# Scores of two attention maps as interleaved 64-row products into two banks, in place of stacked 128-row products

## The chip, the cores and the metric

The kernel runs on one core of one Trainium2 chip. A core has five engines that run their own queues in order and wait for one another through semaphores: PE (TensorE: matmuls, with its weight loads shown apart as PEld), DVE (VectorE), ACT (ScalarE), POOL (GpSimd) and SP (which issues most transfers here). Matmuls write to PSUM, a memory of eight banks of 128 x 512 f32. The metric is the device time of one execution in microseconds (us).

## What is computed

One block of an encoder, on 512 positions of width 1024, in f32. The part that the change touches is the scores of two attentions:

```
# A: 8 heads of 64, chunk-causal with a clipped relative bias per head
scores = einsum(q, k) / sqrt(64) + bias ; probs = softmax(scores) ; o_a = probs @ v
# B: 4 heads, each with two maps of 64 dimensions
s1 = einsum(qa, k1) * scale ; s2 = einsum(qb, k2) * scale
w  = softmax(mask(s1)) - lam * softmax(mask(s2)) ; out = w @ v   (then an RMS norm)
# around them
proj = x @ w_in ; merged = gates * branches ; x = LN1(alpha x + merged @ w_out)
x = LN2(alpha x + relu(x @ w_ff1)^2 @ w_ff2)
```

So a pair of maps is either two heads of A (a head pair p, heads 2p and 2p+1) or the two maps of one head of B. Each map has a contraction of only 64.

## The kernel before

Every f32 operand of a large product is split into a high part, rounded to the matmul type, and a low part, the remainder, and a product is the sum of three matmuls: high by high, high by low, low by high (smm and tmm, L177 to L185). These wide products, 512 columns each, are nearly all of PE's work.

The attention runs inside the projections. `proj` (L647) is a generator that issues the projections in steps; `attn_a` (L328) and `attn_b` (L497) are generators of attention steps, and the loop at L681 to L692 takes one step of attention and then one or two steps of projection. The Tile framework's scheduler then fixes the order of instructions on every engine at build time; at run time each queue is strictly in that order.

A unit of attention is one map and one block t of 128 query rows. Chunk-causality leaves n = 128 (t+1) key columns, so a score matmul has 128, 256, 384 or 512 columns. The chain of a unit: scores on PE into a bank (L266 to L272); DVE adds the bias and takes the row minimum of the negated sum (L278); ACT takes exp and the row sum (L280); DVE the reciprocal (L282); POOL multiplies by it (L372 in A; L575 for the second map in B); three units later PE transposes the block into a bank (L289), ACT copies it as high part ph (L296), DVE forms the low part pl (L297); after the last block of a map the product with v follows (L351 and L352 in A, L511 to L513 in B).

Scores use stacked operands. `stack` (L248) turns a bank that holds 64 rows of one map over 64 rows of another into two tiles: for map e, one half holds the high part and the other half the low part, so a tile of 128 rows is [high; low] of one map. That takes two ACT and two DVE instructions on 64 rows each (L254, L255). `swapped` (L260) makes [low; high] of a q tile by two transfers from SBUF to SBUF (L262, L263). Then scores of one map are two matmuls over all 128 rows: [high; low] by [high; low], and [low; high] by [high; low] (L270, L271), which sum all four products.

The banks (L72): four "mm" for the wide products, one "o" for products with v, and three "st", which both the scores and the transposes of A take in turn (B's transposes go to an mm bank). Later stages use all eight in rotation (L700, L846).

POOL also turns q and k of B by their positions (`rope`, L476 to L485, four instructions for each head and side).

Of the kernel before, what the change touches and what calls it, by code (L numbers as in the profile page):

```python
# [16 lines left out]
P = 128  # L17
S = 512
# [22 lines left out]
def block_kernel(ctx, tc, w, x_t, x, pos, relb, bgate, lq1, lk1, lq2, lk2, subg,  # L41
# [30 lines left out]
    def bank(tag):  # L72
        return psum.tile([P, S], F32, tag=tag, bufs={"mm": 4, "st": 3, "o": 1}[tag], name=name(tag))
# [174 lines left out]
    def stack(ps, scale):  # L248
        res = []
        for e in range(2):  # L250
            t = qp.tile([P, S], FR, tag="q", name=name("q"))
            hs = slice(64 * e, 64 * e + 64)
            ls = slice(64 - 64 * e, 128 - 64 * e)
            A.activation(t[hs], ps[hs], AF.Copy, scale=scale)  # L254
            V.scalar_tensor_tensor(out=t[ls], in0=ps[hs], scalar=scale,  # L255
                                   in1=t[hs].bitcast(F32), op0=ALU.mult, op1=ALU.subtract)
            res.append(t)
        return res

    def swapped(q):  # L260
        t = qp.tile([P, S], FR, tag="q", name=name("q"))
        nc.sync.dma_start(out=t[0:64].bitcast(F32), in_=q[64:128].bitcast(F32))  # L262
        nc.sync.dma_start(out=t[64:128].bitcast(F32), in_=q[0:64].bitcast(F32))  # L263
        return t

    def scores(q1, q2, k1, t):  # L266
        n = (t + 1) * P
        sl = slice(t * P, n)
        ps = st_bank()
        T.matmul(ps[:, :n], q1[:, sl], k1[:, :n], start=True, stop=False)  # L270
        T.matmul(ps[:, :n], q2[:, sl], k1[:, :n], start=False, stop=True)  # L271
        return ps  # L272
# [55 lines left out]
    def attn_a():  # L328
        units = []
        for p in range(4):  # L330
            for e in range(2):
                for t in range(NT):
                    units.append((p, e, t))
# [3 lines left out]
        def finish(u, ex, r):  # L337
            p, e, t = u
            n = (t + 1) * P
# [24 lines left out]
        for i in range(len(units) + LAG + 1):  # L364
            if i < len(units):
                p, e, t = units[i]
                q1, q2, k1 = qk_a[p]
                h = 2 * p + e
                ps = scores(q1[e], q2[e], k1[e], t)
                ex, r = softexp(ps, tbias[h], t)  # L370
                n = (t + 1) * P
                G.tensor_scalar(ex[:, :n], ex[:, :n], r, None, op0=ALU.mult)  # L372
                pend.append((units[i], ex, r))
                if e == 1 and t == NT - 1:
                    qk_a.pop(p)
# [610 lines left out]
```

## Time and profile before

| | |
|---|---|
| median of 3 runs (lowest, highest) | 741.46 us (741.35, 741.72) |
| the profiled execution, its own time | 741.43 us |
| its span in the trace | 739.6 us |
| PE busy | 725.7 us, 98% of the span, 3446 matmuls |
| PEld busy | 606.0 us, 82% |
| DVE busy | 423.4 us, 57% |
| ACT busy | 283.6 us, 38% |
| POOL busy | 94.4 us, 13% |
| granted TensorE clock over the span | 0.997 of full speed |
| transfers q<-q of `swapped` | 32, 128 KB each, 2.3 us median to landing |

How to read it: the profile shows one execution. A matmul's own duration overlaps the next one's, so what a matmul takes from PE is read from the start of one to the start of the next, here called its pitch. A busy engine is not one at its peak, and idle time of an engine that nobody waits for costs nothing. The attention lies between 42 and about 300 us, inside the projections; after that come the branch products, the output product, the two layer norms and the feed-forward part.

### The profile page before, as it was taken

The numbers are of one execution on the slowest core, as the hardware profiler recorded it, in microseconds if no ns is written. First come the engines' busy times: TensorE is split into PE (matmuls) and PEld (weight loads), VectorE is DVE, ScalarE is ACT, GpSimd is POOL, SyncE is SP. The second block draws the span as 40 slices with busy tenths as digits, with TensorE's granted clock in tenths as the row PEclk, the third lists the DMA queues.
The fourth block names the chain that finished last, engine by engine and source line by source line (L and its number), as shares of the span: only waits on it lengthen the run. The fifth ranks groups of instructions, "written<-read, shape, count | busy, mean of one in ns | idle before, by whom it ended". The sixth has DMA issues, their size and how long they took to land.

```text
span 739.6 us, 9267 instructions
## 1 busy us (share of the span) xinstructions
PE 725.7 (98%) x3446; PEld 606.0 (82%) x3446; DVE 423.4 (57%) x831; ACT 283.6 (38%) x497; POOL 94.4 (13%) x127
## 2 busy tenths in 40 slices
PE   8999999999999999999999999999999999999995
PEld 6888888878888888888788888888888888888885
DVE  6566655546666764746876886423135655612545
ACT  5565654536565643224363223221212322312200
POOL 0023333550122121143000000000000000000001
PEclk9999999999999999999999999999999999999998
DMA  8553222212332222182502232322223223232302
GB/s 294 197 173 112 85 88 60 83 58 86 121 108 86 86 63 104 62 313 96 190 1 84 87 114 86 115 86 98 102 86 113 86 86 113 86 113 86 115 29 85
DMA packets 26940, 78.34 MB, mean 106 GB/s; under 512 B 4368, under 2 KB 5136, under 8 KB 26896
## 3 DMA queue, kind: packets, MB, share of 16 engines
q1 hardware_dynamic: 26176, 76.71, 31.3%
q10 hardware_dynamic: 720, 1.05, 0.4%
q8 instruction: 27, 0.44, 0.2%
q14 instruction: 17, 0.14, 0.1%
HBM read 71.45 MB, written 2.10 MB: 99 GB/s over the span
## 4 chain that ended last, share of the span: by engine, by line
PE 87%; DVE 4%; POOL 3%; ACT 2%; DMA 2%; issue 1%; SPq 0%; DVEq 0%; ACTq 0%; POOLq 0%
PE mm L178 11%; PE mm L180 11%; PE mm L179 11%; PE mm L183 7%; PE mm L185 7%; PE mm L184 7%; PE st L185 3%; PE st L184 3%; PE st L183 3%; PE st L180 3%; PE st L179 3%; PE st L178 3%; POOL G L629 2%; DMA raw<-in_w_dram 2%; PE st L271 1%; PE o L185 1%
## 5 line engine op out<-in xcount | busy, mean ns | idle before, releaser
L83 DVE TENSOR_TENSOR wl<-raw,wh 128x1024 fp32r<-128x1024 f32 (+1 forms) x115 | 140.2, 1219 | 128.5 <-ACT wh L82 128.4
L82 ACT CAST wh<-raw 128x1024 fp32r<-128x1024 f32 (+1 forms) x115 | 120.0, 1044 | 207.6 <-PE st L185 67.1
L183 PE MATMUL mm<-wh,X 128*128 128x512 f32 (+1 forms) x192 | 77.0, 401 | 1.9 <-ACT X L82 1.6
L178 PE MATMUL mm<-X,wh 128*128 128x512 f32 x192 | 76.9, 401 | 0.0
L179 PE MATMUL mm<-X,wh 128*128 128x512 f32 x192 | 74.9, 390 | 0.0
L180 PE MATMUL mm<-X,wl 128*128 128x512 f32 x192 | 74.9, 390 | 0.0
L184 PE MATMUL mm<-wl,X 128*128 128x512 f32 (+1 forms) x192 | 74.5, 388 | 0.0
L185 PE MATMUL mm<-wh,X 128*128 128x512 f32 (+1 forms) x192 | 74.2, 388 | 0.0
L783 POOL TENSOR_SCALAR s<-s 128x1 f32<-128x1 f32 x1 | 0.4, 409 | 388.8 <-DVE s L767 388.8
L178 PE MATMUL mm<-x1t_h,wh 128*128 128x512 f32 x128 | 49.8, 389 | 0.0
L179 PE MATMUL mm<-x1t_l,wh 128*128 128x512 f32 x128 | 49.8, 389 | 0.0
L180 PE MATMUL mm<-x1t_h,wl 128*128 128x512 f32 x128 | 49.8, 389 | 0.0
L280 ACT ACTIVATE e<-e,s 128x128 f32<-128x128 f32 (+3 forms) x64 | 36.1, 564 | 30.4 <-DVE s L278 30.0
L372 POOL TENSOR_SCALAR e<-e,s 128x128 f32<-128x128 f32 (+3 forms) x32 | 34.7, 1085 | 76.3 <-DVE s L282 76.3
L183 PEld LDWEIGHTS mm<-wh,X 128*128 128x128 f32 x192 | 36.2, 189 | 9.8 <-ACT X L82 2.7
L185 PEld LDWEIGHTS mm<-wh,X 128*128 128x128 f32 x192 | 36.0, 188 | 7.8 <-DVE X L83 0.3
L180 PEld LDWEIGHTS mm<-X,wl 128*128 128x128 f32 x192 | 36.0, 188 | 7.7
L178 PEld LDWEIGHTS mm<-X,wh 128*128 128x128 f32 x192 | 36.1, 188 | 6.9
L184 PEld LDWEIGHTS mm<-wl,X 128*128 128x128 f32 x192 | 36.2, 188 | 6.7 <-DVE wl L83 0.2
L179 PEld LDWEIGHTS mm<-X,wh 128*128 128x128 f32 x192 | 36.2, 188 | 6.5
L82 ACT CAST V<-lt 128x512 fp32r<-128x512 f32 x24 | 14.9, 621 | 62.8 <-DVE lt L858 62.8
L180 PE MATMUL st<-x1t_h,wl 128*128 128x512 f32 (+1 forms) x104 | 38.8, 373 | 0.0
(257 smaller groups left out, 1537.0 us busy)
## 6 DMA issues: line engine op xcount, KB each, us to landing
raw<-in_w_dram SPq DMA_DIRECT2D x119, 512.0 KB, 3.3
q<-q SPq DMA_DIRECT2D x32, 128.0 KB, 2.3
G<-in_relb_dram SPq DMA_DIRECT2D x8, 256.0 KB, 4.2
x<-in_x_dram SPq DMA_DIRECT2D x4, 512.0 KB, 7.6
e<-in_x_t_dram SPq DMA_DIRECT2D x7, 256.0 KB, 6.4
out_dram<-x SPq DMA_DIRECT2D x3, 256.0 KB, 2.0
out_dram<-x ACTq DMA_DIRECT2D x3, 256.0 KB, 2.1
raw<-in_w_dram SPq DMA_DIRECT2D x2, 256.0 KB, 3.2
```

The source lines that it names most:

```text
L82: A.copy(out=h, in_=src)
L83: (eng or V).tensor_tensor(out=l, in0=src, in1=h.bitcast(F32), op=ALU.subtract)
L178: T.matmul(ps, lw_h, rh, start=first, stop=False)
L179: T.matmul(ps, lw_h, rl, start=False, stop=False)
L180: T.matmul(ps, lw_l, rh, start=False, stop=last)
L183: T.matmul(ps, ah, w_h, start=first, stop=False)
L184: T.matmul(ps, ah, w_l, start=False, stop=False)
L185: T.matmul(ps, al, w_h, start=False, stop=last)
L271: T.matmul(ps[:, :n], q2[:, sl], k1[:, :n], start=False, stop=True)
L280: A.activation(e[:, :n], e[:, :n], AF.Exp, bias=nm, scale=-1.0, accum_out=sums)
L372: G.tensor_scalar(ex[:, :n], ex[:, :n], r, None, op0=ALU.mult)
L629: G.tensor_tensor(out=m, in0=m, in1=g, op=ALU.add)
```

## The change

The scores are written on plain tiles. `parts_of` replaces `stack`: one ACT instruction makes the high part of all 128 rows (map 0 in rows 0 to 63, map 1 in rows 64 to 127) and one DVE instruction the low part. `swapped` and its transfers are gone. `scores` now makes both maps of a pair in one call: three products per map (high by high, high by low, low by high), each over 64 rows, issued in turn, map 0, map 1, map 0 and so on, map 0 into one bank of a new kind "sc" and map 1 into the other. A pair therefore takes six matmuls where it took four. The three st banks become two sc banks and one st bank, which the transposes of A have to themselves.

The order of units in A changes with it: both heads of a pair run together, block by block, and two units are issued at every second step; the product with v comes ahead of the transposes in a step.

```diff
-        return psum.tile([P, S], F32, tag=tag, bufs={"mm": 4, "st": 3, "o": 1}[tag], name=name(tag))
+        return psum.tile([P, S], F32, tag=tag, bufs={"mm": 4, "sc": 2, "st": 1, "o": 1}[tag], name=name(tag))
...
-    def stack(ps, scale):
-        res = []
-        for e in range(2):
-            t = qp.tile([P, S], FR, tag="q", name=name("q"))
-            hs = slice(64 * e, 64 * e + 64)
-            ls = slice(64 - 64 * e, 128 - 64 * e)
-            A.activation(t[hs], ps[hs], AF.Copy, scale=scale)
-            V.scalar_tensor_tensor(out=t[ls], in0=ps[hs], scalar=scale,
-                                   in1=t[hs].bitcast(F32), op0=ALU.mult, op1=ALU.subtract)
-            res.append(t)
-        return res
-
-    def swapped(q):
-        t = qp.tile([P, S], FR, tag="q", name=name("q"))
-        nc.sync.dma_start(out=t[0:64].bitcast(F32), in_=q[64:128].bitcast(F32))
-        nc.sync.dma_start(out=t[64:128].bitcast(F32), in_=q[0:64].bitcast(F32))
-        return t
-
-    def scores(q1, q2, k1, t):
+    def parts_of(ps, scale):
+        h, l = (qp.tile([P, S], FR, tag="q", name=name("q")) for _ in range(2))
+        A.activation(h, ps, AF.Copy, scale=scale)
+        V.scalar_tensor_tensor(out=l, in0=ps, scalar=scale, in1=h.bitcast(F32),
+                               op0=ALU.mult, op1=ALU.subtract)
+        return h, l
+
+    def scores(q, k, t):
+
         n = (t + 1) * P
         sl = slice(t * P, n)
-        ps = st_bank()
-        T.matmul(ps[:, :n], q1[:, sl], k1[:, :n], start=True, stop=False)
-        T.matmul(ps[:, :n], q2[:, sl], k1[:, :n], start=False, stop=True)
+        ps = [bank("sc") for _ in range(2)]
+        for i, (a, b) in enumerate(((0, 0), (0, 1), (1, 0))):
+            for m in range(2):
+                hs = slice(64 * m, 64 * m + 64)
+                T.matmul(ps[m][:, :n], q[a][hs, sl], k[b][hs, :n], start=(i == 0), stop=(i == 2))
         return ps
...
-        units = []
-        for p in range(4):
-            for e in range(2):
-                for t in range(NT):
-                    units.append((p, e, t))
+        units = [(p, t, e) for p in range(4) for t in range(NT) for e in range(2)]
...
-            if i < len(units):
-                p, e, t = units[i]
-                q1, q2, k1 = qk_a[p]
-                h = 2 * p + e
-                ps = scores(q1[e], q2[e], k1[e], t)
-                ex, r = softexp(ps, tbias[h], t)
+            if i < len(units) and i % 2 == 0:
+                p, t, _ = units[i]
                 n = (t + 1) * P
-                G.tensor_scalar(ex[:, :n], ex[:, :n], r, None, op0=ALU.mult)
-                pend.append((units[i], ex, r))
-                if e == 1 and t == NT - 1:
+                for e, ps in enumerate(scores(*qk_a[p], t)):
+                    ex, r = softexp(ps, tbias[2 * p + e], t)
+                    G.tensor_scalar(ex[:, :n], ex[:, :n], r, None, op0=ALU.mult)
+                    pend.append((units[i + e], ex, r))
+                if t == NT - 1:
                     qk_a.pop(p)
+            k = i - LAG - 1
+            if k >= 0 and units[k][1] == NT - 1:
+                p, t, e = units[k]
+                pv(p, e)
             if i >= LAG and i - LAG < len(units):
                 finish(*pend.pop(0))
-            k = i - LAG - 1
-            if k >= 0 and k % NT == NT - 1:
-                p, e, t = units[k]
-                pv(p, e)
             yield
...
-            res.append(stack(ps, 0.125 if which == 0 else 1.0))
-        q1, k1 = res
-        return q1, [swapped(q) for q in q1], k1
+            res.append(parts_of(ps, 0.125 if which == 0 else 1.0))
+        return res
...
-                q1, q2, k1 = ops[h]
-                es = []
-                for m in range(2):
-                    ps = scores(q1[m], q2[m], k1[m], t)
-                    es.append(softexp(ps, maskb, t))
-                (e1, r1), (e2, r2) = es
+                (e1, r1), (e2, r2) = [softexp(ps, maskb, t) for ps in scores(*ops[h], t)]
...
-            r = stack(ps, 0.125 if which == 0 else 1.0)
-            if which == 0:
-                qk_a[p] = [r, [swapped(q) for q in r], None]
-            else:
-                qk_a[p][2] = r
+            qk_a.setdefault(p, []).append(parts_of(ps, 0.125 if which == 0 else 1.0))
```

What stands in the queues, at two places. The first is on PE, at the last block (t = 3) of the last head pair of A, among the wide products of the v projection of B. Names are tiles: q are parts of queries and keys, st, sc, mm and o banks, e a block of probabilities. Before:

```order
L185 MATMUL mm_1575<-wh_1580,X_225 128x512
L270 MATMUL st_1661<-q_941,q_854 128x512
L271 MATMUL st_1661<-q_941,q_860 128x512
L289 MATMUL st_1674<-ident,e_1561 128x128
L351 MATMUL o_1678<-ph_1517,V_327 128x512
```

In the changed kernel, at the same block:

```order
L263 MATMUL sc_1615<-q_912,q_819 128x512
L263 MATMUL sc_1616<-q_912,q_819 128x512
L263 MATMUL sc_1615<-q_913,q_819 128x512
L263 MATMUL sc_1616<-q_913,q_819 128x512
L263 MATMUL sc_1615<-q_912,q_820 128x512
L263 MATMUL sc_1616<-q_912,q_820 128x512
L281 MATMUL st_1639<-ident,e_1448 128x128 x2
L183 MATMUL mm_1576<-wh_1582,X_218 128x512
```

One map's two matmuls became a run of six for two maps, and the transposes behind them go to the one st bank. Of 32 calls, 30 are such a run of six; two are cut by wide products.

The second place is on POOL, where the last units of A meet the rotations of B (L480 to L485 before, L465 to L470 after, four rows for each of eight tiles G). Before, the multiply of the unit (head 7, t = 0) stands among them and those of t = 1 to 3 behind:

```order
L480 TENSOR_TENSOR s_2487<-G_1184,cos_t 128x128
L481 TENSOR_TENSOR s_2488<-G_1184,sin_t 128x8x8
L372 TENSOR_SCALAR e_1561<-e_1561,s_1566 128x128
L483 TENSOR_TENSOR s_2488<-G_1184,sin_t 128x8x8
L485 TENSOR_TENSOR G_1184<-s_2487,s_2488 128x8x16
L480 TENSOR_TENSOR s_2493<-G_1491,cos_t 128x128
L481 TENSOR_TENSOR s_2494<-G_1491,sin_t 128x8x8
L483 TENSOR_TENSOR s_2494<-G_1491,sin_t 128x8x8
L485 TENSOR_TENSOR G_1491<-s_2493,s_2494 128x8x16
L372 TENSOR_SCALAR e_1599<-e_1599,s_1604 128x256
```

In the changed kernel:

```order
L465 TENSOR_TENSOR s_2469<-G_1175,cos_t 128x128
L357 TENSOR_SCALAR e_1554<-e_1554,s_1559 128x384
L466 TENSOR_TENSOR s_2470<-G_1175,sin_t 128x8x8
L468 TENSOR_TENSOR s_2470<-G_1175,sin_t 128x8x8
L470 TENSOR_TENSOR G_1175<-s_2469,s_2470 128x8x16
L465 TENSOR_TENSOR s_2475<-G_1490,cos_t 128x128
L466 TENSOR_TENSOR s_2476<-G_1490,sin_t 128x8x8
L468 TENSOR_TENSOR s_2476<-G_1490,sin_t 128x8x8
L470 TENSOR_TENSOR G_1490<-s_2475,s_2476 128x8x16
L357 TENSOR_SCALAR e_1562<-e_1562,s_1567 128x384
```

The rotations kept their places; the multiply among them is now one of 384 columns (head 6, t = 2), and the next one of 384 columns (head 7, t = 2) stands behind the last rotation, with the two of t = 3 after it.

## Rows read from the trace of the kernel before

**Rows 1.** The page: busy time by engine, and the chain that ended last, by engine.
```profile
PE 725.7 (98%) x3446; PEld 606.0 (82%) x3446; DVE 423.4 (57%) x831; ACT 283.6 (38%) x497; POOL 94.4 (13%) x127
...
PE 87%; DVE 4%; POOL 3%; ACT 2%; DMA 2%; issue 1%; SPq 0%; DVEq 0%; ACTq 0%; POOLq 0%
```

**Rows 2.** Windows: stretch, length, PE, PEld, DVE, ACT, POOL busy, clock, DMA share.
```profile
42.00:140.00 98.00, 97.71 (x491) 82.09 (x490) 61.09 (x157) 55.44 (x129) 32.77 (x32) 1.00 0.31 96
140.00:180.00 40.00, 38.29 (x190) 31.10 (x189) 22.45 (x53) 19.85 (x43) 16.97 (x33) 1.00 0.27 79
180.00:300.00 120.00, 120.00 (x604) 101.86 (x603) 75.45 (x208) 64.02 (x129) 23.87 (x21) 1.00 0.28 88
```

**Rows 3.** Timeline of POOL and PE where A ends and the rotations run.
```profile
140.67 0.46 POOL L480 TENSOR_TENSOR s<-G,cos_t 128x128 f32<-128x128 f32 x1 [0.81 <-ACT G L467]
...
151.32 0.60 POOL L372 TENSOR_SCALAR e<-e,s 128x128 f32<-128x128 f32 x1
...
154.36 3.69 POOL L372 TENSOR_SCALAR e<-e,s 128x256 f32<-128x256 f32 x3
...
151.98 0.33 PE L289 MATMUL st<-ident,e 128*128 128x128 f32 x1 [1.25 <-POOL e L372]
```

**Rows 4.** Timeline of PE: start us, duration us; score matmuls of each width.
```profile
58.48 0.33 PE L270 MATMUL st<-q,q 128*128 128x384 f32 x1
58.65 0.34 PE L271 MATMUL st<-q,q 128*128 128x384 f32 x1
58.83 0.60 PE L289 MATMUL st<-ident,e 128*128 128x128 f32 x4
...
62.02 0.39 PE L270 MATMUL st<-q,q 128*128 128x512 f32 x1
62.25 0.39 PE L271 MATMUL st<-q,q 128*128 128x512 f32 x1
...
66.61 0.22 PE L270 MATMUL st<-q,q 128*128 128x128 f32 x1
66.67 0.28 PE L271 MATMUL st<-q,q 128*128 128x128 f32 x1
66.78 0.41 PE L289 MATMUL st<-ident,e 128*128 128x128 f32 x2
66.95 0.48 PE L178 MATMUL mm<-X,wh 128*128 128x512 f32 x1
67.27 0.39 PE L179 MATMUL mm<-X,wh 128*128 128x512 f32 x1
...
69.77 0.28 PE L270 MATMUL st<-q,q 128*128 128x256 f32 x1
69.88 0.28 PE L271 MATMUL st<-q,q 128*128 128x256 f32 x1
70.00 0.49 PE L289 MATMUL st<-ident,e 128*128 128x128 f32 x3
```

**Rows 5.** Timeline of the weight loads: eight loads of 128 columns, merged.
```profile
226.75 0.97 PEld L524 LDWEIGHTS mm<-ones,e 128*128 128x128 f32 x8
```

**Rows 6.** Groups by shape: the same weight loads; busy us, mean ns of one.
```profile
L524 PEld LDWEIGHTS mm<-ones,e 128*128 128x128 f32 x32 | 4.0, 191 | 0.1
```

**Rows 7.** Groups by shape: POOL's multiply of 384 columns.
```profile
L372 POOL TENSOR_SCALAR e<-e,s 128x384 f32<-128x384 f32 x8 | 10.0, 1245 | 15.7 <-DVE s L282 15.7
```

**Rows 8.** Timeline: one transpose of A, and when its bank is read out.
```profile
128.93 0.49 PE L289 MATMUL st<-ident,e 128*128 128x128 f32 x3
...
129.97 0.56 DVE L297 TENSOR_TENSOR pl<-st,ph 128x384 fp32r<-128x384 f32 x1 [0.41 <-ACT ph L296]
```

**Rows 9.** Groups by shape: the weight split on DVE; the copies of `stack`.
```profile
L83 DVE TENSOR_TENSOR wl<-raw,wh 128x1024 fp32r<-128x1024 f32 x113 | 138.8, 1229 | 125.0 <-ACT wh L82 124.8
...
L254 ACT ACTIVATE q<-mm 64x512 fp32r<-64x512 f32 x32 | 18.9, 590 | 13.6 <-DVE q L255 9.6 <-PE st L271 2.0 <-PE mm L180 1.1
...
L255 DVE SCALAR_TENSOR_TENSOR q<-mm,q 64x512 fp32r<-64x512 f32 x32 | 22.0, 689 | 4.5 <-ACT q L254 3.5
```

More of the change, by code (lines that the diff above doesn't have):

```diff
@@ L337, in finish @@
         def finish(u, ex, r):
-            p, e, t = u
-            n = (t + 1) * P
+            p, t, e = u
             if t == 0:
@@ L699, in block_kernel @@
     early.close()
-    rotation[:] = ["mm", "mm", "mm", "mm", "o", "st", "st", "st"]
+    rotation[:] = ["mm", "mm", "mm", "mm", "o", "sc", "sc", "st"]
     late = ctx.enter_context(tc.tile_pool(name="late", bufs=1))
@@ L845, in block_kernel @@
         pass
-    rotation[:] = ["o", "st", "st", "st", "mm", "mm", "mm", "mm"]
+    rotation[:] = ["o", "sc", "sc", "st", "mm", "mm", "mm", "mm"]
     def x1t(k, lo=0, hi=S):
```

## The prediction, made before the changed kernel was run

> **What bounds the kernel now.** I read the page first, then windows over the attention stage, then the timeline of PE there, and last POOL's timeline at the one place where PE waits. The page shows PE busy for 98% of the span and 87% of the chain that ended last, with DVE at 57%, ACT at 38% and POOL at 13% [rows 1]. So the time is the sum of PE's pitches plus the moments in which PE stands still. The windows say how many of those there are in the stretch that the change touches: PE is busy 97.71 of 98 us from 42 to 140, 38.29 of 40 from 140 to 180 and all of 120 from 180 to 300 [rows 2], so it stands still for 0.3 + 1.7 = 2.0 us. Of these, 1.25 us are one wait for POOL at 151.98, where a transpose wants the block whose multiply stands among the rotations [rows 3]. The clock is granted in full in all three stretches [rows 2], so it has no part in the sum. Everything after 300 us keeps its instructions, and PE is in order, so what the attention stage gains or loses moves the end by as much.
>
> The reader should see from this that removing ACT or DVE work pays next to nothing, and that the change has to be costed in PE pitches.
>
> **What the scores take now.** Pitch is start to start [rows 4]. A map with 128 columns takes 66.78 - 66.61 = 0.17 us for its two matmuls, one with 256 takes 0.23, with 384 takes 0.35, with 512 takes twice 62.25 - 62.02, 0.46. The four blocks of a map take 1.21 us, two maps 2.42 us, and there are eight such pairs (four head pairs of A, four heads of B): 19.4 us in all. This is the whole stake on PE.
>
> A wide matmul hides the load of the next one's weights, a narrow one does not: eight loads in a row, with almost no columns behind them, are 0.97 us from the first start to the last end [rows 5], and one alone shows 0.19 [rows 6], so they follow each other every (0.97 - 0.19) / 7 = 0.11 us. That is the pitch of 256 columns.
>
> **The change part by part.** *The matmuls.* A pair of maps takes six instead of four, over 64 rows each. No row of this kernel has a matmul on less than 128 rows, so the price has to be bounded by what the two halves of the array do at the same time. There are three cases, all from the same pitches.
>
> (a) Both the columns and the loads of the two halves overlap. Then six matmuls are three rounds: 3 x 0.11, 3 x 0.115, 3 x 0.175 and 3 x 0.23 for the four widths, 1.89 us in place of 2.42, a gain of 0.53 x 8 = 4.2 us.
>
> (b) The columns overlap, the loads follow each other. Six loads are 6 x 0.11 = 0.67 us, which is more than the three rounds for 128, 256 and 384 columns and about the same for 512 (0.69). The sum is 3 x 0.67 + 0.69 = 2.70 us, a loss of 0.28 x 8 = 2.2 us. The narrow blocks lose more than the wide ones win.
>
> (c) Nothing overlaps: twice case (a), 3.78 us, a loss of 1.36 x 8 = 10.9 us.
>
> I take (b). In the trace, loads never stand closer than 0.11 us [rows 5, 6], and a wide matmul hides exactly one; six separate loads with little to hide them is what these rows are nearest to.
>
> The Trainium skill speaks on both sides here. TensorE: Matmul & The Clock Gate, section LDWEIGHTS, says that a load takes its columns at 1.2 GHz and no less for fewer rows, 107 ns for 128 columns; the trace agrees for 128 rows (0.11), and no run here shows 64. TensorEngine Tiling (Array Packing), section Key Properties, says that tiles of the array load weights and multiply in parallel, which is case (a). By the first page alone the sum would be (b), by the second it would be (a).
>
> *The change between 128 and 64 rows.* PE now goes from whole-array to half-array work and back around each of 33 stretches of scores (two calls are cut by wide products, so a few more). The nearest row is the other change of mode in this kernel: after transposes the next wide matmul has a pitch of 67.27 - 66.95 = 0.32 instead of 0.23 us, 0.09 more, and going into the transposes costs nothing (a score matmul of 384 columns keeps its 0.18 ahead of them) [rows 4]. In the new order 25 stretches are followed directly by transposes, which pay this 0.09 today already. The other eight add 8 x 0.09 = 0.7 us. The lower bound is 0. The upper one is that PE must run empty each time: a 512-column matmul lasts 0.39 us at a pitch of 0.23 [rows 4], so 0.16 us, 66 times, 10.6 us. I take 0.7, the row nearest to it.
>
> *POOL's place among the rotations.* The rotations keep their places, but the block that waits among them is now 384 columns wide and a second one stands behind them. If the multiply starts at the same 151.32 as today's [rows 3], it ends 1.25 us later [rows 7] at 152.57, where today's 0.60 ended at 151.92: 0.65 us later. PE comes there earlier: between the end of the k projection and this transpose stand 36 wide products before and after; the scores there take 0.67 + 0.69 = 1.36 us in place of 1.21, the transposes ahead are five blocks in place of nine (0.4 us less), so 0.2 us earlier. The wait grows from 1.25 to about 2.1 us. The next multiply follows the other rotations, which took 154.36 - 151.92 = 2.44 us, and ends at 152.57 + 2.44 + 1.25 = 156.3. PE is there after three transposes and twelve wide products, 3.1 us after 152.6, at 155.7, and waits 0.5. Together 2.6 in place of 1.25: +1.4 us. In case (a) PE is 0.15 us earlier still, +1.5; in case (c) a microsecond later, +0.3.
>
> *One st bank for the transposes of A.* A bank is read out 129.97 + 0.56 - 128.93 = 1.6 us after its transpose starts [rows 8]. In the new order at least twelve wide products, 2.75 us, lie between two transposes, so 1.1 us is left over. One weight split on DVE that comes ahead of the read-out takes 1.2 us [rows 9], which uses that up and little more. I take 0, with 2 us as the upper end if two splits line up at several of the 32 turns; then the wide products behind the transpose in PE's queue wait, and with them everything. The sc banks have some 24 wide products, 5.5 us, between calls in most of A: 0.
>
> *The copies and transfers.* 16 ACT instructions of 0.59 and 16 DVE instructions of 0.69 us go [rows 9], 9 and 11 us of engines that PE hardly waits for: 0, and at best the 0.75 us of still PE that is not POOL's wait [rows 2, 3]. The 32 transfers of `swapped` free SP's queue, where weight loads stand behind them; PE does not wait for those weights now [rows 2]: 0.
>
> **The sum** is made against the profiled execution's own 741.43 us, which is the median (741.46) to within 0.03. +2.2 (scores) + 0.7 (change of mode) + 1.4 (POOL) + 0 + 0 = +4.3 us: 745.7 us.
>
> **The rivals.** *Faster: the two halves work independently, loads too* (case (a), change of mode free). -4.2 + 1.5 = -2.7 us: 738.7. For it: the two halves share no rows and no bank, so nothing in the program makes one wait for the other. Against it: the loads in the trace are never closer than 0.11 us [rows 5, 6]. It decides from the point at which two loads take under about 0.17 us together: there the scores cost no more than today with the change of mode paid. POOL's wait eats a third of it. Chance 0.27.
>
> *The halves don't overlap at all*, so the change does not do what it says: +10.9 + 0.7 + 0.3 = +11.9 us, 753.3. For it: the pitches of this kernel's matmuls are those of one queue, each starting when the columns of the one before are through [rows 4]. Against it: all of those use every row of the array, so they could not have overlapped, and the rows don't speak of halves. Chance 0.15.
>
> *PE runs empty at every change between 64 and 128 rows.* As in case (b) plus 10.6 us, with POOL's wait hidden by most of a microsecond in return: +2.2 + 10.6 + 0.6 = +13.4 us, 754.8; with overlapping loads 6.4 us less, 748.4. Against it: the change to transposes costs 0.09 us, not 0.16 twice [rows 4]. The Trainium skill, TensorEngine Tiling (Array Packing), section Key Properties, states such a drain for a change of tiling mode; no row of this kernel can show it. Chance 0.20.
>
> **How the numbers follow.** Forecast 0.38, faster rival 0.27, no overlap 0.15, running empty 0.20. What a measurement of this kernel tells from no change is 0.2%, 1.5 us, so 740.0 to 742.9 is the same. The forecast reaches from 741.5 (no price for the mode, no more wait for POOL) to 749 (the st bank and more of the mode): of its 0.38, 0.02 faster, 0.06 same, 0.30 slower. The faster rival, from 737.2 (POOL's wait hidden) to 741.5: 0.20 faster, 0.07 same. The others are slower whole. Faster 0.22, same 0.13, slower 0.65. The range 737.5 to 756.0 leaves out a sliver of the faster rival and the upper half of running empty with loads in turn, under 0.2 together.
>
> **What would show it.** In the trace of the changed kernel, the starts of six score matmuls of 512 columns: two starts close together and then about 0.23 us until the next two for (a) and (b), an even 0.23 for (c). For 128 columns the whole run of six decides between (a), 0.33 us, and (b), 0.67. The pitch from a wide product into the first score matmul, and from the last one out, against 0.23 shows the price of the mode. The wait for POOL of the transpose of head 6, t = 2 should be about 2.1 us and that of head 7 about 0.5; transposes of A that wait for DVE would show the st bank. The copies on ACT and DVE should be 16 each at 0.6 and 0.7 us, and nobody should gain from the other 16. The prediction is wrong if loads of 64 rows stand closer than those of 128, which is the faster rival, or if the change of mode costs more than a tenth of a microsecond.

## The result, and the profile after

The changed kernel takes 752.84 us (median of 4 runs, 751.21 to 753.94), the kernel before 741.58 us in the same session (741.35 to 741.72): a ratio of 1.015, 95% interval 1.0134 to 1.0167. It is slower, as forecast, but by 11.3 us where 4.3 were forecast. The profiled execution of the changed kernel is its shortest, 751.21 us, 9.8 us more than that of before; its span in the trace is 749.2 us.

The page of the changed kernel (busy us, share, instructions; the chain that ended last, by engine) answers to [rows 1]:

```profile
PE 733.5 (98%) x3510; PEld 599.2 (80%) x3510; DVE 411.3 (55%) x815; ACT 274.9 (37%) x481; POOL 94.9 (13%) x127
...
PE 87%; POOL 4%; DVE 3%; DMA 2%; ACT 2%; issue 1%; SPq 0%; DVEq 0%; ACTq 0%; POOLq 0%
```

PE has 64 products more and is 7.8 us longer busy; ACT and DVE have 8.7 and 12.1 us less to do, and nobody gains by that. The windows of the changed kernel (columns as in [rows 2]):

```profile
42.00:140.00 98.00, 97.97 (x508) 76.59 (x507) 53.85 (x147) 50.11 (x118) 31.64 (x32) 1.00 0.23 76
140.00:180.00 40.00, 36.96 (x185) 28.45 (x183) 21.08 (x44) 18.85 (x38) 18.01 (x32) 1.00 0.19 56
180.00:300.00 120.00, 119.60 (x615) 95.58 (x616) 69.00 (x209) 59.72 (x125) 24.47 (x22) 1.00 0.22 74
```

PE hardly stands still between 42 and 140 us, so the one st bank costs nothing there; it stands still for 3.0 us instead of 1.7 where the rotations run, and for 0.4 us behind 180 us, where it did not before. Next, PE's timeline of the changed kernel around stretches of scores (start us, duration us; x6 is the six half products of a call, merged), which answers to [rows 4]:

```profile
46.08 0.62 PE L263 MATMUL sc<-q,q 64*128 64x256 f32 x6
46.63 0.50 PE L178 MATMUL mm<-X,wh 128*128 128x512 f32 x1
46.97 0.40 PE L179 MATMUL mm<-X,wh 128*128 128x512 f32 x1
...
58.68 0.39 PE L179 MATMUL mm<-X,wh 128*128 128x512 f32 x1
58.90 0.39 PE L180 MATMUL mm<-X,wl 128*128 128x512 f32 x1
59.22 0.96 PE L263 MATMUL sc<-q,q 64*128 64x512 f32 x6
60.12 0.44 PE L281 MATMUL st<-ident,e 128*128 128x128 f32 x2
...
66.02 0.39 PE L180 MATMUL mm<-X,wl 128*128 128x512 f32 x1
66.34 0.55 PE L263 MATMUL sc<-q,q 64*128 64x128 f32 x6
66.82 0.55 PE L281 MATMUL st<-ident,e 128*128 128x128 f32 x3
```

Two things stand there. Six products of 512 columns take 60.12 - 59.22 = 0.90 us, against 1.38 for six pitches of 0.23, so the halves do run side by side. Six of 128 columns take 66.82 - 66.34 = 0.48 us, which lies between the 0.33 of the prediction's case (a) and the 0.67 of its case (b), so the single starts have to decide. In the trace's single starts the two products of a round are 3 to 4 ns apart, and so are their weight loads; rounds follow each other every 0.235, 0.168, 0.116 and 0.113 us for 512, 384, 256 and 128 columns. That is case (a) of the prediction, and not case (b), which it took. But the ends of the stretch are dear: the wide product ahead of it has a pitch of 59.22 - 58.90 = 0.32 instead of 0.23, the first and the last round are each some 0.1 us longer than those between them, and a wide product that follows directly has 46.97 - 46.63 = 0.34.

The weight loads of the changed kernel show why (same columns):

```profile
58.68 0.19 PEld L180 LDWEIGHTS mm<-X,wl 128*128 128x128 f32 x1
59.22 0.53 PEld L263 LDWEIGHTS sc<-q,q 64*128 64x128 f32 x6 [0.35 <-issue]
```

The load for a wide product runs during the product ahead of it (58.68 for the one at 58.90). The load for the first half product starts at 59.22, with the half product itself, 0.32 us behind the start of the wide one. At this change nothing is loaded ahead. The Trainium skill, TensorEngine Tiling (Array Packing), section Key Properties, states both sides of this: tiles load and multiply independently, and a change of tiling mode drains the engine. The trace agrees with the first (starts and loads 3 to 4 ns apart) and fits the second (0.32 us instead of 0.23 ahead of the first half product, and its load not before it).

### The profile page after: what moved, and what is told of

The parts are those of the page before. It is cut to its first block, busy times and chain, and to the rows that moved or that the text cites. A ratio compares the mean times of both kernels' runs of the same rounds, so it can differ in the third digit from the quotient of the medians.

```text
span 749.2 us, 9269 instructions
## 1 busy us (share of the span) xinstructions
PE 733.5 (98%) x3510; PEld 599.2 (80%) x3510; DVE 411.3 (55%) x815; ACT 274.9 (37%) x481; POOL 94.9 (13%) x127
## 4 chain that ended last, share of the span: by engine, by line
PE 87%; POOL 4%; DVE 3%; DMA 2%; ACT 2%; issue 1%; SPq 0%; DVEq 0%; ACTq 0%; POOLq 0%
PE mm L178 11%; PE mm L180 11%; PE mm L179 11%; PE mm L183 7%; PE mm L185 7%; PE mm L184 7%; PE sc L263 3%; PE sc L183 2%; PE sc L184 2%; PE sc L185 2%; DMA raw<-in_w_dram 2%; PE sc L179 2%; PE sc L178 2%; PE sc L180 2%; POOL G L608 2%; PE st L281 1%
## 5 line engine op out<-in xcount | busy, mean ns | idle before, releaser
L184 PE MATMUL mm<-wl,V 128*128 128x512 f32 (+1 forms) x80 | 30.3, 379 | 0.0
```

The source lines that it names most:

```text
L184: T.matmul(ps, ah, w_l, start=False, stop=False)
```

## Experiments: what the loss hangs on

The theory now (M): the halves overlap wholly, but each change between whole and half rows lets PE run empty and leaves the loads at both ends uncovered, some 0.3 us for each of 33 stretches. Rival B: order and banks cost the time. Rival R: a product over 64 rows is slow by itself.

**Whole rows in the new order.** Order, banks and tiles stay, the products change:

```diff
-        for i, (a, b) in enumerate(((0, 0), (0, 1), (1, 0))):
+        for i, (a, b) in enumerate(((0, 0), (0, 1))):
             for m in range(2):
-                hs = slice(64 * m, 64 * m + 64)
-                T.matmul(ps[m][:, :n], q[a][hs, sl], k[b][hs, :n], start=(i == 0), stop=(i == 2))
+                T.matmul(ps[m][:, :n], q[a][:, sl], k[b][:, :n], start=(i == 0), stop=(i == 1))
```

> The changed kernel with its order, its banks and its plain tiles, but each map as two products over all 128 rows instead of three over 64 (so each score adds both maps' rows and leaves one product out; the time is that of four whole matmuls per pair of maps, as before the change, in the new order). Theory M (the halves overlap, but each change between whole and half rows lets PE run empty, 0.3 to 0.4 us for each of 33 stretches): the loss goes except for POOL's longer wait, 741.6 + 1.3 = 742.9 us, 741.5 to 744.5, and the wide product ahead of a stretch is back at a pitch of 0.23. Rival B (order and banks: one st bank, two sc banks in turn, the multiplies' place): still 750 or more. Rival R (every product over 64 rows is slow by itself): as M, so this run tells B from the other two.

Measured: 744.18 us, ratio 1.0024 (1.0014 to 1.0033). So B falls: nearly all of the loss goes with the half rows. The run is still 1.3 us above the 742.9 that M expected, which the section on the pauses explains.

**Six whole products**, the same with all three products per map over 128 rows:

> As the run of four whole matmuls, but with six over 128 rows per pair of maps (each score adds both maps' rows). By the pitches of before a third product per map is half of 19.4 us more, 9.7 us: M and R both give 742.9 + 9.7 = 752.6 us, 751 to 754.5, that is, about what the halves take; if the halves had brought nothing at all and no change of rows cost anything, the changed kernel would be this one. Rival B: 758 or more.

Measured: 754.11 us, 1.0162 (1.0139 to 1.0186), as expected. By the pitches of [rows 4], six whole products would be 29.1 us for all calls and three rounds of halves 15.2; some three quarters of that gain go back at the ends of the stretches.

**Two rounds instead of three**, the half rows kept:

```diff
-        for i, (a, b) in enumerate(((0, 0), (0, 1), (1, 0))):
+        for i, (a, b) in enumerate(((0, 0), (0, 1))):
...
-                T.matmul(ps[m][:, :n], q[a][hs, sl], k[b][hs, :n], start=(i == 0), stop=(i == 2))
+                T.matmul(ps[m][:, :n], q[a][hs, sl], k[b][hs, :n], start=(i == 0), stop=(i == 1))
```

> The changed kernel with two of the three rounds of half products per call (the low part of q times the high part of k is left out). Theory M: a round costs only its pitch of 0.113, 0.116, 0.168 or 0.235 us by width, 8 x 0.63 = 5.1 us less, 747.7 us, 746.5 to 749; the two ends of a stretch stay as long as they are, so four half matmuls still take 5 us more than four whole ones. Rival R (the price hangs on each product): a third of the 22.4 us inside the stretches and of the some 5.5 us at their ends goes, 9.3 us, 743.5 us.

Measured: 744.86 us, 1.003 (1.0019 to 1.0041), between the two expectations, which therefore does not decide. The sums below do.

**Fewer stretches.** Blocks 0 and 2 of a head share a bank and are issued together:

```diff
+TS = (0, 2, 1, 3)
...
-        units = [(p, t, e) for p in range(4) for t in range(NT) for e in range(2)]
+        units = [(p, t, e) for p in range(4) for t in TS for e in range(2)]
...
+                if t != 2:
+                    ts = (0, 2) if t == 0 else (t,)
+                    ready.update(zip(ts, scores(*qk_a[p], ts)))
...
```

> The changed kernel with the blocks in the order 0, 2, 1, 3, and the scores of blocks 0 and 2 (128 and 384 columns, one bank together) issued as one stretch of twelve: the same number of products in 25 stretches instead of 33. Theory M: eight stretches less at 0.3 to 0.4 us, 2.4 to 3.2 us less, 750.0 us, 749 to 751.5. Rival R: no change, 752.8. Rival B: no change but for POOL's waits among the rotations, 751.5 to 754.

Measured: 750.09 us, 1.0097 (1.008 to 1.0114). The same products in 25 stretches cost 2.75 us less than in 33 by the medians: M's 2.4 to 3.2, against 0 for R. That the medians meet M so well is in part luck. By the traces the attention stage is 4.1 us shorter (table below); 0.6 of this are shorter pauses at the rotations, and 1.2 a wait for an sc bank that this order does not have. Some 2.3 us are left for eight stretches, 0.29 each; far behind the stage a longer pause (3.69 us instead of 2.62, described below) takes some of it back.

The pitches of PE, summed from the starts of its products in each trace over the 840 wide products of the attention stage (us; a pitch is start to start; a pause is what a pitch ahead of a transpose or inside the product with v, pv, has over the usual one). The changed kernel has 33 stretches because 31 of the 32 calls are issued whole and one is cut in two; the section on the change has two cut, which the trace does not bear out.

| | before | whole, four | changed | two rounds | whole, six | merged |
|---|---|---|---|---|---|---|
| stretches of scores | 50 | 33 | 33 | 33 | 33 | 25 |
| score products, sum | 21.52 | 20.50 | 22.36 | 16.45 | 31.20 | 20.23 |
| wide product ahead, mean | 0.236 | 0.232 | 0.321 | 0.319 | 0.236 | 0.318 |
| 120 transposes, sum | 9.72 | 10.08 | 11.01 | 11.00 | 9.82 | 10.86 |
| pauses at the rotations | 1.9 | 3.4 | 3.1 | 3.4 | 2.8 | 2.5 |
| whole stage | 251.60 | 254.45 | 259.75 | 255.38 | 263.06 | 255.67 |

The changed kernel and the one with four whole products have the same order, so their difference, leaving out the pauses and what the clock behind them costs, is the price: scores +1.86, wide products ahead 33 x 0.09 = +2.96, and behind the stretches transposes +0.93, pv +0.30, preparation +0.18, wide products +0.37. That is +6.6 us. Three rounds at their steady pitches would be 4.2 us cheaper than four whole products, so the changes of rows cost 6.6 + 4.2 = 10.8 us, 0.33 us a stretch. Some 0.7 of this is not theirs: at 179 us, where B starts, PE waits inside a call for the second sc bank, and that stretch has 1.2 us more than others of its width, against 0.5 in the run with four whole products. Without it the price is 10.1 us, 0.31 a stretch. The two-round run gives the same: its scores are 5.9 us below the changed kernel's, of which 0.8 is this wait, so a round costs the 5.1 us that M said, while the wide products ahead stay at 0.32 and the transposes behind at 11.0. My expectation for its time was wrong mainly because it started from the changed kernel's median, which holds a later pause (2.62 us, here 1.33) and the lower clock behind it.

**The price by itself.** In the kernel before, one product more at the head of each of the 64 maps' scores, over all rows (the control, first line) or over half of them (second line):

```diff
+        T.matmul(ps[:, :P], q1[:, sl], k1[:, :P], start=True, stop=True)
...
+        T.matmul(ps[:, :P], q1[0:64, sl], k1[0:64, :P], start=True, stop=True)
```

> The kernel before, with one product more at the head of each of its 64 maps' scores: all 128 rows, 128 columns, into the same bank, whose numbers the next product writes over. Control for the run with half the rows. Both theories: 64 x 0.11 = 7.2 us more than before, 748.9 us, 747.5 to 750.

> The same, but the product that is added uses 64 of the 128 rows, so that PE goes from whole rows to half rows and back 64 times, with one half product in between. Theory M (a price for each stretch of half products, 0.28 to 0.34 us both ways, whatever is in it): 64 x 0.3 = 19 us more than the control, 768 us, 765 to 771. Rival R (the price hangs on each half product: 10.8 us over 192 of them, 0.056 each): 3.6 us more than the control, 752.5 us. If only one way costs (0.09 going in): 5.8 us, 754.7.

Measured: 748.93 us for the control (1.009, 1.0073 to 1.0108) and 768.82 us for half the rows (1.0357, 1.0339 to 1.0375). The 64 visits cost (768.82 - 748.93) / 64 = 0.31 us each, M's figure; R's 752.5 falls. By the traces it is a little more: the attention stage is 278.20 - 258.90 = 19.3 us longer, and the control still pauses 2.0 us at the rotations and just behind them, where the run with half rows, which comes later, does not; together 0.33 us each. PE's timeline of the control, then of the run with half rows, at the same scores of 256 columns:

```profile
55.23 0.39 PE L180 MATMUL mm<-X,wl 128*128 128x512 f32 x1
55.46 0.22 PE L270 MATMUL st<-q,q 128*128 128x128 f32 x1
55.52 0.33 PE L271 MATMUL st<-q,q 128*128 128x256 f32 x1
55.69 0.28 PE L272 MATMUL st<-q,q 128*128 128x256 f32 x1
55.81 0.49 PE L290 MATMUL st<-ident,e 128*128 128x128 f32 x3
```

```profile
57.60 0.39 PE L180 MATMUL mm<-X,wl 128*128 128x512 f32 x1
57.92 0.32 PE L270 MATMUL st<-q,q 64*128 64x128 f32 x1
58.17 0.38 PE L271 MATMUL st<-q,q 128*128 128x256 f32 x1
58.40 0.28 PE L272 MATMUL st<-q,q 128*128 128x256 f32 x1
58.51 0.49 PE L290 MATMUL st<-ident,e 128*128 128x128 f32 x3
```

From the wide product to the transposes it is 55.81 - 55.23 = 0.58 us and 58.51 - 57.60 = 0.91 us. Of the 0.33, 0.09 lie ahead of the half product, 0.19 between it and the whole one, and 0.06 on the whole one behind.

**What the second half brings.** Both maps' products on the same 64 rows, and the three of one map ahead of the three of the other:

```diff
-                hs = slice(64 * m, 64 * m + 64)
+                hs = slice(0, 64)
```

> The changed kernel with both maps' products on rows 0 to 63 (the second map's numbers come from the first map's rows), so that no two products can run side by side. Theory M: a round of two takes two pitches instead of one, 3 x 0.63 x 8 = 15.2 us more than the changed kernel, 768 us, 765 to 771, and the ends of the stretches cost as much as now. Rival (the halves only hide each other's loads, or do nothing for each other): 752.8 to 758.

```diff
-        for i, (a, b) in enumerate(((0, 0), (0, 1), (1, 0))):
-            for m in range(2):
+        for m in range(2):
+            for i, (a, b) in enumerate(((0, 0), (0, 1), (1, 0))):
```

> The changed kernel with the three products of one map first and then the three of the other, each on its own half. Theory M: only the last product of the first map and the first of the second run side by side, five pitches for six products instead of three, 2 x 0.63 x 8 = 10.1 us more than the changed kernel, 762.9 us, 760 to 766. Rival (PE looks past the products of one half and issues those of the other): 752.8.

Measured: 764.22 us on one half (1.0294, 1.0273 to 1.0315), just under the range expected, and 754.44 us for one map after the other (1.0162, 1.0139 to 1.0185). In the first the score products' pitches are 37.14 us in all, 14.8 more than the changed kernel's, for the 15.2 expected; the medians differ by less, 11.4 us: PE pauses 1.2 us less at the rotations, and what the later pause and the clock behind it cost differs from execution to execution. The second contradicts what I expected of M: the order of issue makes no difference to the scores. Here a stretch of 512 columns in each, first on one half, then one map after the other:

```profile
60.02 0.39 PE L180 MATMUL mm<-X,wl 128*128 128x512 f32 x1
60.33 1.66 PE L263 MATMUL sc<-q,q 64*128 64x512 f32 x6
61.92 0.44 PE L281 MATMUL st<-ident,e 128*128 128x128 f32 x2
```

```profile
60.05 0.39 PE L180 MATMUL mm<-X,wl 128*128 128x512 f32 x1
60.37 0.97 PE L263 MATMUL sc<-q,q 64*128 64x512 f32 x6
61.27 0.44 PE L281 MATMUL st<-ident,e 128*128 128x128 f32 x2
```

1.59 us on one half, 0.90 for one map after the other, as in the changed kernel. In the single starts of the latter the products come in pairs 10 ns apart, the pairs 0.34 and 0.24 us apart. Two products on the same rows are 0.22 us apart or more in the run on one half, so a pair is one product of each half: the fourth product issued, the other half's first, starts 10 ns behind the first and 0.3 us ahead of the second. Each half behaves as a queue of its own.

## Experiments: the pauses

**POOL.** The timeline of the changed kernel at the rotations, POOL, DVE and PE, answers to [rows 3]:

```profile
153.97 1.24 POOL L357 TENSOR_SCALAR e<-e,s 128x384 f32<-128x384 f32 x1
155.27 0.55 PE L281 MATMUL st<-ident,e 128*128 128x128 f32 x3 [1.41 <-POOL e L357]
157.93 4.46 POOL L357 TENSOR_SCALAR e<-e,s 128x384 f32<-128x384 f32 x3
159.21 0.17 DVE L274 RECIPROCAL s<-s 128x1 f32<-128x1 f32 x1 [3.20 <-POOL e L357]
159.29 0.54 DVE L289 TENSOR_TENSOR pl<-st,ph 128x384 fp32r<-128x384 f32 x1
159.97 0.52 PE L281 MATMUL st<-ident,e 128*128 128x128 f32 x3 [1.42 <-DVE pl L289]
```

The first wait is the multiply itself. The second is put down to DVE: the one st bank is read out only at 159.29, because that read-out stands in DVE's queue behind a reciprocal that waits for POOL. The multiply that PE needs ends at about 157.93 + 1.24 = 159.17, so by this estimate some 0.8 us of the wait belong to the single bank. Taking the last head pair's multiplies off POOL removes both, in either kernel:

```diff
-                G.tensor_scalar(ex[:, :n], ex[:, :n], r, None, op0=ALU.mult)
+                (V if p == 3 else G).tensor_scalar(ex[:, :n], ex[:, :n], r, None, op0=ALU.mult)
```

> The same in the changed kernel, where PE waits twice for POOL's multiplies, 1.57 us each: 3.1 us less than the changed kernel if the waits are POOL's, and another 0.5 to 1.5 in the executions in which PE's clock falls after a wait: 749.2 us, 748 to 750. Rival: the wait passes to DVE: 752.8.

> The kernel before, with the multiplies of the last head pair's exponentials by their reciprocals on DVE instead of POOL, whose queue holds the rotations. In the trace of before PE waits 1.3 us there, and 0.5 us behind it. If the wait is POOL's: 1.5 to 1.9 us less, 739.9 us. Rival: DVE has the copies of q and k before it and PE waits as long: 741.6.

Measured: 747.87 us for the changed kernel so altered (1.0073, 1.0053 to 1.0093), a little less than expected, and 739.75 us for the kernel before (0.9969, 0.9957 to 0.998). In both traces the pauses at the rotations are gone. The second is the fastest version here, 0.3% below the kernel before. With no POOL wait in either, the change costs 747.87 - 739.75 = 8.1 us, of which 1.0 is the later pause described below (2.56 against 1.54 us in the two traces).

The run with four whole products and that with two rounds reach these transposes earlier, and their two waits become one of 3.4 us. The windows of the two-round run (columns as in [rows 2]; the eighth figure is the granted clock) show what follows:

```profile
150.00:155.00 5.00, 1.77 (x9) 1.16 (x8) 1.60 (x5) 0.66 (x3) 4.69 (x10) 1.00 0.30 107
155.00:160.00 5.00, 5.00 (x19) 4.04 (x20) 0.62 (x2) 1.01 (x4) 4.92 (x7) 0.66 0.01 3
160.00:165.00 5.00, 5.00 (x26) 4.00 (x25) 2.39 (x3) 1.88 (x3) 0.65 (x1) 1.00 0.30 105
```

Behind the long pause the granted clock is 0.66 for 5 us, which is part of the time at 1.2 GHz instead of 2.4, and PE starts 19 products where it starts 26 later. In the run with four whole products the windows from 150 to 155 and from 155 to 160 us have 0.81 and 0.85, and its wide products there take 1.1 us more than their usual pitches. With a pause that is 0.3 us longer, this is the 1.3 us that it has above its expectation.

**The pause far behind the change.** Of the 9.8 us between the profiled executions, 259.75 - 251.60 = 8.15 lie in the attention stage. The rest arises at 374 us, where not one instruction was changed: the first transposes of the normalised rows wait longer for ACT. PE's timeline there of before and of the changed kernel (L817 and L792 are the same line):

```profile
367.14 1.09 PE L817 MATMUL mm<-ident,lt 128*128 128x128 f32 x8 [0.97 <-ACT lt L805]
```

```profile
377.03 1.09 PE L792 MATMUL mm<-ident,lt 128*128 128x128 f32 x8 [2.62 <-ACT lt L780]
```

> The changed kernel again, unaltered, for what differs from execution to execution: the wait of 2.6 us ahead of the first transposes of the normalised rows at 373 us, where before had 1.0. Theory W1 (it depends on how the weight transfers happen to fall): it differs by half a microsecond or more from the first profile's. Theory W2 (it is set by the program's order and PE's lateness): 2.5 to 2.8 again. The time: 752.8 us, 751 to 754.

Measured: 753.58 us (1.015, 1.0129 to 1.0171), and a wait of 3.03 us, so neither theory exactly. The attention stage takes 259.75 us again, to the hundredth; what differs from execution to execution is this wait and the clock behind it. Windows of this second profile:

```profile
370.00:375.00 5.00, 3.85 (x17) 2.84 (x16) 4.93 (x8) 0.00 (x0) 0.00 (x0) 1.00 0.32 102
375.00:380.00 5.00, 3.12 (x12) 2.83 (x13) 3.52 (x11) 2.21 (x6) 0.00 (x0) 0.58 0.23 93
```

From these transposes to the last product it takes 367.0 us here and 364.3 in the first profile. That is most of what lies between the executions of 751.2 to 751.6 us (mean granted clock 0.997 and 0.998) and those of 752.5 to 753.9 (0.993 to 0.995).

What makes the wait longer? ACT waits for DVE, and DVE for a chain of weight splits that starts when one weight transfer has landed. Up to that transfer ACT's splits in before and in the changed kernel agree within 0.25 us, measured from the same product of PE; it lands 1.9 us later. Of the changed kernel, the instruction fetch in the window from 358 to 362 us (queue, packets, MB, share of the 16 DMA engines' time) and the weight transfer, alone in the window of its issue, 357.5 to 358.1 us (the last figure is the us to landing); then the same transfer of before, 349.5 to 350.1 us, where no fetch stands beside it:

```profile
q8 instruction: 1, 0.02, 2.1%
...
raw<-in_w_dram SPq DMA_DIRECT2D x1, 512.0 KB, 5.4
```

```profile
raw<-in_w_dram SPq DMA_DIRECT2D x1, 512.0 KB, 3.2
```

In the changed kernel 16 KB of instructions are fetched in the middle of the weight transfer, as one packet that takes 2.1% of 16 engines for 4 us, 1.3 us of one of them. The page counts 27 such fetches on that queue, and they come about every 128 products of PE; 64 products more ahead of this place move them. In all thirteen traces that I had by then the wait was 2.4 to 3.7 us where this fetch met that transfer (seven traces) and 0.95 to 1.54 where it did not (six). The Trainium skill, Runtime: NRT & Kernel Launch, section Instruction fetch mechanics, describes such blocks of 16 KB, 256 instructions, on a DMA queue of the engine's own, and calls their cost mostly hidden; the trace agrees on the size (0.44 MB in 27), and adds that the data transfer beside the fetch lands later. To see whether it is the cause, products were added to the warm-up at the start, which shifts the fetches: 24 in the changed kernel (below), 44 in the kernel before.

```diff
             T.matmul(ps, src[:, 0:P].bitcast(FR), src.bitcast(FR), start=True, stop=True)
+        for _ in range(24):
+            T.matmul(ps[:, 0:64], src[:, 0:P].bitcast(FR), src[:, 0:64].bitcast(FR), start=True, stop=True)
```

> The changed kernel with 24 products of 64 columns more in the warm-up, so that every later instruction of PE lies 24 products further on in its stream. In the changed kernel's trace a transfer of 16 KB of PE's instructions runs at the moment at which one weight transfer that the first normalised rows wait for is on its way; in before it runs 10 us later. Theory W3 (it is this meeting that makes PE pause 2.8 to 3.2 us ahead of the first x1 transposes instead of 1.1 to 1.7, and its clock fall in some executions): the instructions come some 5.5 us earlier, the pause is 1.7 us or less, and the time 752.8 - 1.5 - 2 x (share of executions with the fall) + up to 2.6 for the added products where nothing hides them: 749.5 to 752.5 us. Rival: the pause stays 2.8 to 3.2 us whatever the place of the instruction transfer, 752.8 to 755.4 us.

> The reverse in the kernel before: 44 products of 64 columns more in the warm-up bring its transfer of PE instructions some 10 us forward, onto the same weight transfer. Theory W3: the pause ahead of the first x1 transposes grows from 1.1 us to about 2.8, 1.6 us more, besides up to 4.8 us for the added products at the start, and PE's clock may fall behind it. Rival: the pause stays 1.1 to 1.7.

Measured: 755.93 us (1.0158, 1.0121 to 1.0195) and 751.51 us (1.0116, 1.0085 to 1.0146); the added products delay the start by 3.9 and 8.5 us, more than I expected, and their executions spread over 5 us (751.61 to 756.42 and 748.93 to 753.93), which stays unexplained, so the waits decide and not the times. PE's timeline of the shifted kernel before:

```profile
376.99 1.09 PE L819 MATMUL mm<-ident,lt 128*128 128x128 f32 x8 [2.35 <-ACT lt L807]
```

Its fetch (window from 358 to 362 us) and the same weight transfer (357.8 to 358.4 us):

```profile
q8 instruction: 1, 0.02, 1.6%
...
raw<-in_w_dram SPq DMA_DIRECT2D x1, 512.0 KB, 5.1
```

With the fetch brought onto the transfer, the kernel before waits 2.35 us instead of 0.97, its scores and everything else unchanged. In the shifted changed kernel PE's timeline reads:

```profile
362.38 0.50 PE L183 MATMUL mm<-wh,X 128*128 128x512 f32 x1 [0.44 <-ACT wh L82]
363.64 0.51 PE L184 MATMUL mm<-wl,X 128*128 128x512 f32 x1 [0.76 <-DVE wl L83]
381.72 1.09 PE L794 MATMUL mm<-ident,lt 128*128 128x128 f32 x8 [1.66 <-ACT lt L782]
```

The wait falls from 2.62 to 1.66, but the fetch, some 6 us earlier, now meets the weights of another product, and PE waits 1.2 us for those. So the cause is the meeting of a fetch with a transfer that PE will soon need, and shifting only chooses the transfer. How long PE pauses goes by how late that transfer lands: in the eight traces with a meeting it lands 5.06 to 6.45 us after its issue, and PE's pause, 2.35 to 3.69 us, is each time that figure less 2.6 to 2.8 us; in the seven without one it lands after 3.1 to 3.8 us. Why a fetch delays one landing by more than another stays open.

## Why the prediction was wrong in size

The direction and the bounding view held: PE is the sum of its pitches, and ACT's and DVE's savings brought nothing. Step by step:

- **What the scores take now**, 2.42 us for two maps: right to 1.1 us: the run with four whole products has 20.5 us for the eight pairs of maps, where the sum said 19.4.
- **Scores, +2.2, case (b)**: wrong. The loads of two halves overlap too; rounds go at the steady pitches of case (a), -4.2 us. The rows on which (b) rested [rows 5, 6] are loads over all 128 rows, and say nothing of two halves. Nor do loads never stand closer than 0.11 us in that trace: those of transposes follow each other every 0.06 us (at 52.17 us, for one). In the changed kernel a round of 128 columns comes every 0.113 us, so within a half the spacing of those rows holds, and not across the halves.
- **Change between 128 and 64 rows, +0.7**: wrong, and the step that made the miss. It took the change to transposes, 0.09 us, as the nearest row. That change keeps all 128 rows in use. The change of rows costs some 10.1 us, 0.31 for each stretch, and 0.31 to 0.33 where it was tried by itself. The upper bound of 10.6 was nearly reached, though its working (0.16 us at either end) is not how it divides: 0.09 us lie ahead of the stretch and the rest on its first and last products and behind them.
- **POOL's place, +1.4**: right in size, in part by luck: PE stands still 3.0 us instead of 1.7, +1.3. The split is not right: 2.1 and 0.5 were forecast, 1.4 and 1.4 were seen, and some 0.8 of the second belongs to the st bank.
- **One st bank, 0**: right but for the one place where DVE's queue waits for POOL, some 0.8 us, which is within the 2 us kept for it. The sc banks, also put at 0, cost one wait where B starts, 1.2 us by the pitches; the kernel before waited some 0.5 there for its preparation.
- **Copies and transfers, 0**: right.
- **Everything behind 300 us keeps its instructions, so it moves as a whole**: wrong by 1.65 us. The instructions are the same, their fetches are not at the same place.

The sum of what was measured is 6.6 (halves against whole products, 0.7 of it the sc bank) + 1.3 (the pauses at the rotations) + 1.65 (the later pause) = 9.6 of the 9.8 us between the profiled executions; the median is 1.6 us further, which goes with the lower clock in three of four executions. Of the rivals, running empty with overlapping loads, 748.4, had the mechanism right. It was 2.8 us short of the profiled execution, of which 1.65 are the later pause and 0.7 the pauses at the rotations, which it let grow by 0.6 only. I gave it a fifth, and there to the variant with loads in turn, because a row for another change of mode was cheap. The pair of errors partly cancelled: +2.2 for -4.2 in the scores, +0.7 for some +10.1 at the ends.

## What to carry to other kernels

Half-array products pay by the round and cost by the stretch: here a stretch of six saves 0.13 us on average against four whole products and costs some 0.31 to enter and leave, so by this estimate, which no run tried, stretches have to be about two and a half times as long before the halves win. A row that stands in for something the trace does not show has to share the property in question (here, how many rows are in use), otherwise the upper bound is the better guess. And on a kernel that is 98% busy, a wait cut somewhere else (0.3% by moving eight multiplies off POOL) was worth more than the rewrite.

## What had not been expected of the hardware

- Two halves of the array behave as two queues: products issued three of one half and then three of the other run as fast as those issued in turn (0.90 us for six of 512 columns, against 1.59 on one half). The Trainium skill, TensorE: Matmul & The Clock Gate, section The mechanism, says that matmuls start and end strictly in program order; here the other half's first product, the fourth issued, starts ahead of the second, so the measurement speaks against it for products on different rows.
- Going from whole rows to half rows and back costs some 0.3 us, for one product in between (0.31 to 0.33) as for six (0.31).
- A fetch of 16 KB of instructions beside one 512 KB weight transfer goes with a landing 5.1 to 6.5 us after its issue instead of 3.1 to 3.8, and, where it was moved onto that transfer, with a PE pause of 1.4 us more. So a change in the number of instructions can cost time far behind the place of the change.
- Behind some pauses of PE the granted clock falls for some 5 us: a window has 0.66 behind the 3.4 us at the rotations of the two-round run, 0.58 behind the 3.0 us at the normalised rows in the second profile of the changed kernel (a loss of 2.7 us). Behind 2.6 us in its first profile it did not fall, behind 2.5 us in the run with one map after the other it did (0.68), so the pause's length alone doesn't tell.
